# Projection products of 512 columns, issued as two matmuls of 256

## The chip, the cores and the metric

The kernel runs on one core of one Trainium2 chip. The metric is the device time of one execution in microseconds (us), and less is better. Timed runs of the kernel before gave 1808.48, 1810.51 and 1814.37 us; the median is 1810.51.

## What is computed

The program is a small encoder trunk of two layers over two requests of 512 tokens each, with 1024 features in float32. Layer 0 is differential attention, layer 1 is retention in both directions. Each layer normalizes its input, multiplies it by one wide matrix (the input projection), mixes over the tokens head by head, weighs the result with a gate and multiplies it by an output matrix. The change concerns the input projections alone:

```python
def diff_attention(h, w_in, lq1, lk1, lq2, lk2, subln_g, w_out, lambda_init):
    B, S, _ = h.shape
    proj = h @ w_in                      # 1024 x 8192
    q, k, v, gate = jnp.split(proj, [DA_QK_WIDTH, 2 * DA_QK_WIDTH, 2 * DA_QK_WIDTH + D_INNER], axis=-1)
    ...
def bidir_retention(h, w_in, decay_fwd, decay_bwd, subln_g, w_out):
    B, S, _ = h.shape
    proj = h @ w_in                      # 1024 x 6144
    q, k, v, gate = jnp.split(proj, [RET_QK_WIDTH, 2 * RET_QK_WIDTH, 2 * RET_QK_WIDTH + D_INNER], axis=-1)
    ...
```

## The kernel before

**Precision.** Matmuls run in a shortened float32 format (`float32r`). To keep the accuracy, each operand is split into a high and a low part, and each product is made of three passes, high by high, high by low and low by high: `PASSES = ((0, 0), (0, 1), (1, 0))`, where the first number picks the part of the projection weight and the second the part of the activations.

**Seven products instead of eight.** A projection is done in units, each over a block of columns of the weight and both requests. A unit multiplies blocks of two by two with seven products (`P1` to `P7`, in the order of `SEQ`) in place of eight. The activation side of them, sums and differences of the normalized inputs, is made once for a layer by `make_b` and stays in 28 slots (`Bop`): most lie in one large tile named `arena`, some in tiles of their own, which the profile shows as `b`. The weight side is made for each unit and product by `prep`: ScalarE casts the high part (line 400), VectorE subtracts for the low part (line 403), both into a `ws` tile.

**Two kinds of units.** In a *wide* unit (the value projections) the activations are the stationary operand and the weight moves past them: 128x256 matmuls in the function `wide` (line 609 of the kernel before). In a *pair* unit (queries, keys and gates) the weight is stationary, 128x128, and the activations move: one matmul of 512 columns fills a whole PSUM bank. One product of a pair unit is 4 blocks of the contraction times 3 passes, 12 matmuls of 512 columns in the function `pair` (line 599). There are 24 pair units in layer 0 and 16 in layer 1, so 40 x 7 = 280 such products. The banks they fill carry the names `pj`, `sc` and `o`. Each matmul instruction comes with its own load of the stationary operand, which the profile shows on a row of its own, PEld.

**Stages.** First comes layer 0's projection (to about 640 us), then the attention heads with layer 0's output projection (to about 1020 us), then layer 1's projection (to about 1500 us), then retention with the output projection. In the attention and retention stages other functions issue matmuls: scores (line 1116, 512 columns), attention weights times values (line 1181, 256 columns), the retention products (lines 1315, 1339, 1359, 1367, 256 columns) and the output projection (line 891, 512 columns). Lines 1028, 1040 and 1161 are transposes.

**Order.** Nothing is issued when it is written down. Every step is recorded with an engine, a cost and what it reads and writes (`plan.op`); `Plan.arrange` then simulates the engines by these costs and writes out the order on each of them. A pair product is one step of TensorE with a cost of 2.79:

```python
                    pe(2.79, lambda: pair(ps), reads, [ps])
```

In the first two units the product `P1` is issued as four steps of one contraction block each, at a cost of 0.7. A semaphore then ties a product to what it reads and to those who read its bank.

Of the kernel before, what the change touches and what calls it, by code (L numbers as in the profile page):

```python
# [253 lines left out]
def trunk_kernel(  # L254
# [7 lines left out]
    nc = tc.nc  # L262
# [90 lines left out]
    def bank(tag, name=None):  # L353
        return Buf(plan, tag, BUFS[tag], lambda i: view(pj if tag == "pj" else sc, tag, i, S, [P, S]))
# [35 lines left out]
    def pe(cost, fn, r, w, wait=0.0):  # L390
        plan.op("PE", cost, fn, r, w, wait=wait)
# [126 lines left out]
    class Unit:  # L518
# [67 lines left out]
        def product(self, op):  # L586
            which = BANK_OF[op]
            n_banks = 2 if self.wide else 1
            opens = op in OPENS
            if opens:  # L590
                self.banks[which] = [bank(self.tags[which], which) for _ in range(n_banks)]
            a, b = self.ops.pop(op), B_OF[op]
            bt = [Bop[b, k] for k in range(4)]
            reads = [q[1] for q in a] + bt

            def pair(ps, ks=range(4)):
                for k in ks:
                    for i, (u, v) in enumerate(PASSES):
                        nc.tensor.matmul(  # L599
                            ps.t, a[u][0]()[:, k, :], bt[k][:, v, :], start=(opens and k == 0 and i == 0),  # L600
                            stop=(k == 3 and i == 2), skip_group_check=True)

            def wide(ps, t):
                if self.led and op == "P1" and t == 0:
                    for j in range(NT):
                        nc.tensor.transpose(ps[:, j * P:(j + 1) * P], ident.t, ident.t)
                for k in range(4):
                    for i, (u, v) in enumerate(PASSES):
                        nc.tensor.matmul(  # L609
                            ps[:, (t % 2) * 256:(t % 2) * 256 + 256], bt[k][:, v, t * P:(t + 1) * P],  # L610
                            a[u][0]()[:, k, :], start=(opens and t % 2 == 0 and k == 0 and i == 0),
                            stop=(k == 3 and i == 2), skip_group_check=True)

            if not self.wide:
                ps = self.banks[which][0]
                if op == "P1" and self in first_units[:2]:
                    for k in range(4):
                        pe(0.7, lambda k=k: pair(ps, (k,)), reads[:2] + [bt[k]], [(ps, k)])
                else:
                    pe(2.79, lambda: pair(ps), reads, [ps])  # L620
                return
            for t in range(NT):
                ps = self.banks[which][t // 2]
                led = self.led and op == "P1" and t == 0
                pe(1.87 if led else 1.43, lambda ps=ps, t=t: wide(ps, t), reads + [ident] * led, [ps])
# [827 lines left out]
    for i in range(N2 + 1):  # L1453
        if i < N2:
            b, c = chunks[i]
# [78 lines left out]
```

## The time and the profile before

| | |
|---|---|
| timed runs, median (lowest, highest) | 1810.51 us (1808.48, 1814.37) |
| span of the profiled execution, first to last instruction | 1807.0 us |
| TensorE matmuls | 10299, busy 1794.9 us (99%) |
| weight loads | 10299, busy 1558.1 us (86%) |
| VectorE | busy 1477.1 us (82%) |
| ScalarE | busy 895.1 us (50%) |
| GpSimd | busy 169.5 us (9%) |
| DMA | 328.81 MB, mean 182 GB/s |

The profiled execution has no other time than its span; the timed runs are separate executions. Matmuls are pipelined: one starts before the one before it has ended, so the mean duration in a row (392 ns for 512 columns) is longer than the distance from start to start. A row of the timeline gives the start of a group, the time that it covers, and the count; the distance from start to start is taken from the start of one row to the start of the next.

### The profile page before, as it was taken

How to read it: one execution, taken by the hardware profiler on the slowest of the kernel's cores; microseconds unless marked ns; L12 is line 12 of the kernel's file. 1: busy time of each engine (PE TensorE's matmuls, PEld its weight loads, DVE VectorE, ACT ScalarE, POOL GpSimd, SP SyncE). 2: the span in 40 equal slices, each digit the busy share in tenths (PEclk: the TensorE clock that was granted, in tenths of full speed). 3: DMA queues.
4: the chain of work that ended last, by engine and by line, in shares of the span. 5: the costliest groups of instructions: out<-in, count | busy, mean ns of one | idle time of the engine just before them, and what ended most of it. 6: DMA issues, size and time to landing. Idle time of an engine off the chain costs nothing.

```text
span 1807.0 us, 27780 instructions
## 1 busy us (share of the span) xinstructions
PE 1794.9 (99%) x10299; PEld 1558.1 (86%) x10299; DVE 1477.1 (82%) x2319; ACT 895.1 (50%) x1856; POOL 169.5 (9%) x323
## 2 busy tenths in 40 slices
PE   9999999999999999999999999999999999999998
PEld 6789889898988888888888888898989898888887
DVE  7958787778699888888888897787887967888887
ACT  7753444433434565554555866444434355444346
POOL 1000000000000022222322300000000000111113
PEclk9999999999999999999999999999999999999999
DMA  6444455555545685444554524464657559765662
GB/s 217 134 126 137 161 140 178 184 168 155 174 126 175 201 334 198 178 156 159 190 204 140 190 73 146 140 210 146 205 156 228 151 170 396 272 238 182 225 218 94
DMA packets 162767, 328.81 MB, mean 182 GB/s; under 512 B 12724, under 2 KB 76872, under 8 KB 162632
## 3 DMA queue, kind: packets, MB, share of 16 engines
q1 hardware_dynamic: 162304, 326.71, 54.1%
q8 instruction: 81, 1.33, 0.3%
q14 instruction: 54, 0.44, 0.1%
q10 hardware_dynamic: 328, 0.34, 0.1%
HBM read 209.55 MB, written 117.44 MB: 181 GB/s over the span
## 4 chain that ended last, share of the span: by engine, by line
PE 93%; DVE 2%; DMA 2%; ACT 2%; issue 1%; POOL 0%; SPq 0%; POOLq 0%; DVEq 0%; ACTq 0%
PE pj L599 20%; PE pj L891 19%; PE sc L599 10%; PE pj L609 10%; PE o L599 8%; PE o L1181 5%; PE sc L1116 5%; PE sc L609 5%; PE o L609 2%; PE o L1359 2%; PE tp L1161 2%; PE sc L1315 1%; PE o L1367 1%; PE tp L1339 1%; DMA raw<-in_ret_w_out_dram 1%
## 5 line engine op out<-in xcount | busy, mean ns | idle before, releaser
L891 PE MATMUL pj<-ws,arena 128*128 128x512 f32 x1542 | 391.2, 397 | 0.0
L891 PEld LDWEIGHTS pj<-ws,arena 128*128 128x128 f32 x1542 | 277.7, 188 | 52.7
L599 PE MATMUL pj<-b,ws 128*128 128x512 f32 x1080 | 265.0, 392 | 0.0
L599 PEld LDWEIGHTS pj<-b,ws 128*128 128x128 f32 x1080 | 201.4, 188 | 43.0
L403 DVE TENSOR_TENSOR ws<-st,ws 128x512 fp32r<-128x512 f32 (+1 forms) x192 | 147.9, 774 | 74.8 <-ACT ws L400 56.7
L896 DVE SCALAR_TENSOR_TENSOR b<-pj,crr,b 128x512 f32<-128x512 f32 (+1 forms) x257 | 189.9, 744 | 21.4 <-PE pj L891 21.0
L403 DVE TENSOR_TENSOR ws<-raw,ws 128x512 fp32r<-128x512 f32 (+1 forms) x164 | 141.5, 868 | 71.3 <-ACT ws L400 61.0
L400 ACT CAST ws<-st 128x512 fp32r<-128x512 f32 (+1 forms) x192 | 132.4, 693 | 121.4 <-PE pj L599 36.4
L599 PE MATMUL sc<-arena,ws 128*128 128x512 f32 x768 | 186.8, 392 | 0.0
L599 PE MATMUL o<-arena,ws 128*128 128x512 f32 x744 | 180.0, 393 | 1.1 <-ACT m L385 0.6
L599 PEld LDWEIGHTS sc<-arena,ws 128*128 128x128 f32 x768 | 144.0, 188 | 31.3
L400 ACT CAST ws<-raw 128x512 fp32r<-128x512 f32 (+1 forms) x164 | 125.7, 772 | 87.0 <-PE o L599 45.0
L599 PEld LDWEIGHTS o<-arena,ws 128*128 128x128 f32 x744 | 138.4, 188 | 31.7 <-DVE arena L463 1.4
L599 PE MATMUL pj<-arena,ws 128*128 128x512 f32 x648 | 160.3, 392 | 0.4 <-DVE arena L463 0.4
L599 PEld LDWEIGHTS pj<-arena,ws 128*128 128x128 f32 x648 | 120.8, 188 | 26.7 <-DVE arena L463 0.7
L1134 ACT ACTIVATE b<-sc,nm 128x512 f32<-128x512 f32 x128 | 88.0, 689 | 66.9 <-DVE nm L1124 66.5
L636 ACT COPY c<-pj 128x512 f32<-128x512 f32 x104 | 60.9, 586 | 119.7 <-PE pj L599 66.4
L609 PE MATMUL pj<-ws,b 128*128 128x256 f32 x960 | 116.8, 276 | 0.0
L609 PEld LDWEIGHTS pj<-ws,b 128*128 128x128 f32 x960 | 113.2, 188 | 0.7
L1116 PE MATMUL sc<-arena 128*128 128x512 f32 x384 | 101.2, 395 | 0.3 <-ACT b L1134 0.3
L1181 PEld LDWEIGHTS o<-arena 128*128 128x128 f32 x768 | 93.1, 188 | 2.7
L1181 PE MATMUL o<-arena 128*128 128x256 f32 x768 | 93.7, 278 | 0.0
(207 smaller groups left out, 2855.9 us busy)
## 6 DMA issues: line engine op xcount, KB each, us to landing
qk<-os SPq DMA_DIRECT2D x192, 256.0 KB, 3.6
arena<-qk SPq DMA_DIRECT2D x96, 512.0 KB, 5.8
raw<-in_da_w_in_dram SPq DMA_DIRECT2D x64, 512.0 KB, 5.1
v<-os SPq DMA_DIRECT2D x64, 512.0 KB, 4.3
arena<-v SPq DMA_DIRECT2D x64, 512.0 KB, 4.1
raw<-in_ret_w_in_dram SPq DMA_DIRECT2D x48, 512.0 KB, 4.8
os<-g SPq DMA_DIRECT2D x32, 512.0 KB, 7.4
g<-e SPq DMA_DIRECT2D x48, 256.0 KB, 4.6
```

Of the source, the lines that this page charges most:

```text
L400: act(n, lambda: nc.scalar.copy(dst(), src()), r, w)
L403: dve(n, lambda: nc.vector.tensor_tensor(dst(), src(), hi().bitcast(F32), op=ALU.subtract), r, w)
L599: nc.tensor.matmul(ps.t, a[u][0]()[:, k, :], bt[k][:, v, :], start=(opens and k == 0 and i == 0), stop=(k == 3 and i == 2), skip_group_che ...
L609: nc.tensor.matmul(ps[:, (t % 2) * 256:(t % 2) * 256 + 256], bt[k][:, v, t * P:(t + 1) * P], a[u][0]()[:, k, :], start=(opens and t % 2 == ...
L636: act(S, lambda c=c, ps=ps: nc.scalar.copy(c.t, ps.t), [ps], [c])
L891: nc.tensor.matmul(ps[:, here], o[a][:, e, t * P:(t + 1) * P], u[b][:, e, here], start=(m == 0), stop=(m == 5))
L896: axpy(n, lambda half=half, here=here, ps=ps: nc.vector.scalar_tensor_tensor(half, ps[:, here], rr[:, t % 2:t % 2 + 1], half, op0=ALU.mult ...
L1116: nc.tensor.matmul(s.t, q[:, a, t * P:(t + 1) * P], k[:, b, :], start=(n == 0), stop=(n == 2))
L1134: act(840, lambda j=j, s=s, m=m: nc.scalar.activation(p[:, j, :], s.t, AF.Exp, bias=m.t, accum_out=sm[:, 2 * j + n:2 * j + n + 1]), [s, m] ...
L1161: nc.tensor.transpose(tp[:, j * P:(j + 1) * P], p[:, 0, j * P:(j + 1) * P], ident.t)
L1181: nc.tensor.matmul(o[:, e * 256:(e + 1) * 256], v[b][:, j, e * P:(e + 1) * P], aT[a][:, j, :], start=(n == 0), stop=(n % 12 == 11), skip_g ...
L1359: nc.tensor.matmul(o[:, e * 256:(e + 1) * 256], v_[v][:, 2 * c + j, e * P:(e + 1) * P], a_[:, u, j * 256:(j + 1) * 256], start=(e == 0 and ...
```

## The change

Each matmul of 512 columns of a pair product is issued as two of 256 columns, the left half of the bank and the right half behind each other, both with the same stationary weight. Only the very first of them clears the bank. The recorded cost of the step and all else stays as it was. The lines behind the edit have numbers higher by three in the changed kernel, and the matmul itself stands in line 601 there.

```diff
             def pair(ps, ks=range(4)):
                 for k in ks:
                     for i, (u, v) in enumerate(PASSES):
-                        nc.tensor.matmul(
-                            ps.t, a[u][0]()[:, k, :], bt[k][:, v, :], start=(opens and k == 0 and i == 0),
-                            stop=(k == 3 and i == 2), skip_group_check=True)
+                        for c in range(2):
+                            here = slice(c * 256, (c + 1) * 256)
+                            nc.tensor.matmul(
+                                ps[:, here], a[u][0]()[:, k, :], bt[k][:, v, here],
+                                start=(opens and k == 0 and i == 0 and c == 0),
+                                stop=(k == 3 and i == 2), skip_group_check=True)
```

## The prediction

> **What bounds the kernel now.** I read the busy times first, then the chain that ended last, then the waits of TensorE, then the timeline of single stretches.
>
> ```profile
> span 1807.0 us, 27780 instructions
> PE 1794.9 (99%) x10299; PEld 1558.1 (86%) x10299; DVE 1477.1 (82%) x2319; ACT 895.1 (50%) x1856; POOL 169.5 (9%) x323
> PEclk9999999999999999999999999999999999999999
> ...
> PE 93%; DVE 2%; DMA 2%; ACT 2%; issue 1%; POOL 0%; SPq 0%; POOLq 0%; DVEq 0%; ACTq 0%
> ```
>
> TensorE is busy for 99% of the span, and 93% of the chain that ended last is TensorE. Its granted clock is full in every slice. There are as many weight loads (PEld) as matmuls, 10299 of each. The waits of TensorE on others, longest first in total, are no more than 1.4 us in any row:
>
> ```profile
> PE sc L1010 <- DVE minus L411: 1.4, 1, 1.4
> PE tp L1028 <- DVE arena L463: 1.0, 2, 0.7
> ```
>
> So what counts is the pitch of the matmuls, from start to start; the mean duration of one overlaps with the next and can't be added up. In the groups by line with shapes kept apart, the matmuls that the change touches are all of line 599:
>
> ```profile
> L599 PE MATMUL pj<-b,ws 128*128 128x512 f32 x1080 | 265.0, 392 | 0.0
> L599 PE MATMUL sc<-arena,ws 128*128 128x512 f32 x768 | 186.8, 392 | 0.0
> L599 PE MATMUL o<-arena,ws 128*128 128x512 f32 x744 | 180.0, 393 | 1.1 <-ACT m L385 0.6 <-DVE arena L463 0.3
> L599 PE MATMUL pj<-arena,ws 128*128 128x512 f32 x648 | 160.3, 392 | 0.4 <-DVE arena L463 0.4
> L599 PE MATMUL sc<-b,ws 128*128 128x512 f32 x120 | 29.1, 391 | 0.0
> ```
>
> That is 1080 + 768 + 744 + 648 + 120 = 3360 matmuls of 512 columns, 280 products of 12. Their pitch is read from a stretch of the timeline that holds nothing else. Between these rows lie 16 further products of 12 (two of them shown as 6 + 6):
>
> ```profile
> 207.10 2.91 PE L599 MATMUL sc<-arena,ws 128*128 128x512 f32 x12
> ...
> 253.79 2.91 PE L599 MATMUL pj<-b,ws 128*128 128x512 f32 x12
> 256.54 2.91 PE L599 MATMUL o<-arena,ws 128*128 128x512 f32 x12
> ```
>
> From 207.10 to 256.54 are 18 products, 216 matmuls in 49.44 us: **228.9 ns each**. That holds while VectorE is at 94% (below), so it is TensorE's own pace.
>
> **The change, part by part.** Each of the 3360 matmuls becomes two of 256 columns, with the same stationary tile `ws`, the two halves of the moving tile, and the two halves of the bank. It adds 3360 matmuls and 3360 weight loads (13659 of each after it). Whether the loads of equal weights are merged can be read off what is there: the first two passes of a product already use the same high part of the weight, and the page still counts a load for each matmul. So I take it that each half loads.
>
> The order of the other instructions is the same on every engine in the changed program, since the planner's cost of a product, 2.79, is left as it was. Nothing is moved past a queue and no wait is added; only the time of the 280 products can change.
>
> The trace shows the new shape already. The wide units (line 609) issue 128x256 matmuls with a new weight for each, in the same stages and at the same background of the other engines:
>
> ```profile
> 303.18 5.60 PE L609 MATMUL sc<-ws,arena 128*128 128x256 f32 x48
> 308.62 0.84 PE L609 MATMUL pj<-ws,b 128*128 128x256 f32 x6
> ...
> 314.06 5.60 PE L609 MATMUL sc<-ws,arena 128*128 128x256 f32 x48
> 319.50 5.60 PE L609 MATMUL pj<-ws,b 128*128 128x256 f32 x48
> ```
>
> From 303.18 to 308.62 are 48 of them in 5.44 us, and from 314.06 to 319.50 again 48 in 5.44 us: **113.3 ns each**, so 226.7 for two halves against 228.9 for the whole. But there is a second pitch for this shape. The products of attention weights with values (line 1181) run at one of two paces, with the same shape and the same two tiles:
>
> ```profile
> 707.12 2.99 PE L1181 MATMUL o<-arena 128*128 128x256 f32 x24
> 709.95 1.56 PE L1116 MATMUL sc<-arena 128*128 128x512 f32 x6
> ...
> 719.37 2.90 PE L1181 MATMUL o<-arena 128*128 128x256 f32 x24
> 722.10 1.08 PE L1116 MATMUL sc<-arena 128*128 128x512 f32 x4
> ```
>
> The first group takes 2.83 us for 24, **117.9 ns each**; the second 2.73 us, 113.8. And in the retention stage, two lines in which, as here, two matmuls behind each other use the same weight:
>
> ```profile
> 1594.42 0.86 PE L1339 MATMUL tp<-arena 128*128 128x256 f32 x6
> 1595.12 0.87 PE L1315 MATMUL sc<-arena 128*128 128x256 f32 x6
> 1595.82 1.54 PE L891 MATMUL pj<-ws,arena 128*128 128x512 f32 x6
> ```
>
> Both take 0.70 us for 6, 116.7 ns each, in groups too short to settle. Neither row has TensorE waiting, so the slower pace lies in how a weight load and the running matmul get on with each other. Which pace the new products keep is the whole question, and the trace of before can't show it: there the stationary tile is `ws` and the moving one is the arena or `b`, at 512 columns only.
>
> The bounds for a pair of halves are thus 226.7 and 2 x 117.9 = 235.8 ns against 228.9: a gain of 2.2 or a loss of 6.9 ns for each old matmul. Of the 3360, those of the start don't set the pace:
>
> ```profile
> core 0: us, PE busy (x) PEld busy (x), PEclk, DMA share, GB/s
> 0.00:50.00 50.00, 29.59 (x120) 21.89 (x120) 1.00 0.57 196
> ```
>
> These 120 fall in the first 50 us, where TensorE has gaps before new operands. I count the other 3240. The fast pace gives 3240 x 2.2 ns = -7.2 us, the slow one 3240 x 6.9 ns = +22.4 us. **I take the fast pace**: line 609 is the nearest row, being in the same stages, with the same two kinds of tiles in changed roles, and its pace holds: from 303.18 to 319.50 it issues 144 matmuls (eight groups of 6 lie between the rows) in 16.32 us. Only its first 48 behind a product of line 599 take 0.03 us longer, in the chain in order of time:
>
> ```profile
> 297.87 5.47 PE o L609 x48
> 303.34 5.44 PE sc L609 x48
> ```
>
> Such a crossing stays in one form or another, some 24 times: at most 0.7 us either way, which I leave at nothing.
>
> What covers the rest? The other engines first: a faster TensorE asks more of VectorE. The windows of a stretch of pair products alone and of one of mostly wide products:
>
> ```profile
> 500.00:600.00 100.00, 100.00 (x439) 82.04 (x438) 93.96 (x152) 40.12 (x71) 0.00 (x0) 1.00 0.48 143
> 299.00:327.00 28.00, 28.00 (x241) 27.63 (x239) 19.66 (x31) 12.20 (x21) 0.00 (x0) 1.00 0.57 175
> ```
>
> The columns after the length are the busy times of PE, PEld, DVE, ACT and POOL. VectorE has 6 us free in 100, and TensorE would take 1 us less for the same work, so it stays ahead; were that cover gone, no more than the 7.2 us of gain would go with it. The loader is at 82% in the first stretch and at 99% in the second: line 609 runs at 113.3 ns with the loader filled, so a filled loader is no bar by itself. Does its reading slow others? The same VectorE operation in both stretches, pair products first:
>
> ```profile
> L403 DVE TENSOR_TENSOR ws<-st,ws 128x512 fp32r<-128x512 f32 x21 | 14.4, 685 | 1.3 <-ACT ws L400 0.8
> ...
> L403 DVE TENSOR_TENSOR ws<-st,ws 128x512 fp32r<-128x512 f32 x3 | 2.0, 682 | 0.0
> ```
>
> 685 and 682 ns: no. And the fetching of 6720 more instructions:
>
> ```profile
> q8 instruction: 81, 1.33, 0.3%
> ```
>
> The columns are packets, MB, and their share of the time of 16 engines. 81 packets of 16 KB are, if they are TensorE's 10299 loads and as many matmuls, some 250 instructions each. At two instructions in 113.3 ns a packet lasts 14 us, and 0.3% of 16 engines' span is 1.1 us for each: hidden, at nothing. If it weren't, each of some 26 new packets would cost about that 1.1 us, 29 us in all; the 144 matmuls of line 609 above are more than a packet holds and pass without a gap, so I don't count it.
>
> The sum against the profiled execution: 1807.0 - 7.2 = 1799.8 us of span. The median of the runs, 1810.51, lies 3.5 us above the span, for what is around it and the spread of runs (1808.48 to 1814.37). So 1810.5 - 7.2 = **1803.3 us**.
>
> **The rivals.**
>
> *The slow pace* (slower). A load that starts just behind the start of a matmul and reads at the same time holds that matmul up by 4.6 ns, at every one of them, since each half now has a load beside its whole length, where a 512-column matmul has the second part of its length free of it. Place: every pair product in both projection stages. For it: line 1181 keeps 117.9 over a whole group of 24, and lines 1315 and 1339, which repeat a weight as the halves do, are above 113.3. Against it: line 609, with a load beside every matmul too, falls back to 113.3 each time. It decides from a mean pitch of 114.4 ns, half of 228.9. Price: +22.4 us, **1832.9 us**. I give it 0.20.
>
> *A price for each matmul in between*, by changing between both paces or by a small start-up cost of each instruction: a mean of (113.3 + 117.9) / 2 = 115.6 ns, 231.2 for two, 2.3 more than now, x 3240 = +7.5 us: **1818 us**. For it: the 116.7 ns of the two retention lines. Against it: two matmuls of line 609 cost less than one of line 599, which leaves no room for a price per instruction. I give it 0.17.
>
> The Trainium skill speaks for this one: "TensorE: Matmul & The Clock Gate", section "Back-to-back issue gap", gives a warm matmul N / 2.4 + 2.5 ns, so a fixed part that twice as many matmuls pay twice. By that rule (an estimate from its figures) the halves would cost 2.5 ns more than the whole, 3240 times, +8.1 us, 1818.6 us. The trace disagrees on both lengths: 228.9 where the rule has 215.8, and 113.3 where it has 109.2, and the difference that it makes has the other sign.
>
> *No change*: the second half goes without its load, or the pitch is per column after all. Two matmuls at half of 228.9 each: 1810.5 us. For it: 226.7 and 228.9 are within 1%. Against it: loads of equal weights are not merged now. 0.05.
>
> **How the numbers follow.** The fast pace keeps 0.58. About 0.3%, 5.4 us, is what a measurement of this kernel can tell from no change. The gain of 7.2 us is only 1.8 us beyond that, less than the spread of the runs, so I put one in six of the fast case within it: faster 0.48; within 0.3% 0.10 + 0.05 = 0.15; slower 0.20 + 0.17 = 0.37. The fast case alone would be 1800 to 1806. The range has to reach to the others, until little is left out: from 1800 to the slow pace and a little spread above, 1834.
>
> **What would show it right or wrong.** Right: 13659 matmuls and loads; a product of 24 halves in 2.72 us from start to start in the middle of a stretch, where it was 2.75; the loader near 100% in 500 to 600 us; no new waits of TensorE; the lines of the attention and retention stages as before. Slow pace: 2.83 us a product in long stretches. In between: some stretches at 2.72 and others at 2.83. Wrong in another way: new idle time before the loads (instructions or operands late), or a longer mean of the VectorE operations beside the filled loader.

## The result, and the profile after

The changed kernel takes 1825.70 us (median of 5, 1825.36 to 1827.21), the kernel before in the same comparison 1808.48 us (median of 5, 1808.26 to 1814.37). The ratio is 1.0093, with a 95% interval of 1.0081 to 1.0104: slower by 17 us, where 7 us faster was forecast. The profiled execution has a span of 1823.4 us, 16.4 more than before; the granted clock is 0.999 in both.

From the page of the changed kernel, the span, the busy times, the queue that brings the instructions, and the chain by engine:

```profile
span 1823.4 us, 34495 instructions
...
PE 1812.6 (99%) x13659; PEld 1716.5 (94%) x13659; DVE 1478.1 (81%) x2319; ACT 895.6 (49%) x1856; POOL 170.0 (9%) x323
...
q8 instruction: 107, 1.75, 0.4%
...
PE 93%; DVE 2%; DMA 2%; ACT 1%; issue 0%; POOL 0%; SPq 0%; POOLq 0%; DVEq 0%; ACTq 0%
```

TensorE is still what counts, with the 13659 matmuls and loads that were foreseen. Its longest wait is the one of before, and VectorE's operation beside the pair products takes what it took; a row of the waits, and one of the groups from 500 to 600 us:

```profile
PE sc L1013 <- DVE minus L411: 1.4, 1, 1.4
```

```profile
L403 DVE TENSOR_TENSOR ws<-st,ws 128x512 fp32r<-128x512 f32 x21 | 14.4, 685 | 3.9 <-ACT ws L400 3.7
```

So the time went into the pitch, the distance from one matmul's start to the next one's. Two pieces of the timeline of the changed kernel, both with nothing but pair products (columns: start, time covered, engine, line, operation, count):

```profile
213.60 2.99 PE L601 MATMUL pj<-b,ws 128*128 128x256 f32 x24
216.42 2.99 PE L601 MATMUL pj<-arena,ws 128*128 128x256 f32 x24
219.25 2.99 PE L601 MATMUL pj<-b,ws 128*128 128x256 f32 x24
...
506.54 2.88 PE L601 MATMUL pj<-b,ws 128*128 128x256 f32 x24
509.26 2.88 PE L601 MATMUL pj<-arena,ws 128*128 128x256 f32 x24
511.98 2.88 PE L601 MATMUL pj<-b,ws 128*128 128x256 f32 x24
```

From 213.60 to 219.25 are 48 halves in 5.65 us, 117.7 ns each (117.8 over longer pieces); from 506.54 to 511.98 are 48 in 5.44 us, 113.3 ns each. Same line, tiles of the same names, VectorE busy for 85% beside both pieces: **two paces, each held for a long stretch**. Going through all starts of the trace, 4944 of the 6720 halves belong to stretches at 117.8 ns and 1776 to stretches at 113.3. Where a stretch changes its pace stands in the chain in order of time (start, length, engine, bank, line, count; L612 are the wide products):

```profile
158.37 5.66 PE pj L612 x48
164.03 2.83 PE pj L601 x24
166.86 5.45 PE o L612 x48
...
188.63 5.44 PE pj L612 x48
196.79 5.66 PE pj L612 x48
202.45 2.83 PE o L601 x24
```

The wide product at 158.37 is slow (5.66 for 48) and so is the pair product behind it (2.83 for 24). The next wide product, at 166.86, is fast (5.45) and stays so. Between the end of the row at 188.63 (194.07) and 196.79 lies a pair product of 2.72, fast as well; and the wide one behind that, at 196.79, is slow again, as is the pair product at 202.45. So, in this trace, **the pace goes over unchanged from wide to pair, and turns into the other one from pair to wide**. In the whole of it 24 of 24 entries into pair products keep the pace, and 20 of 23 entries into wide ones turn it (the three others lead to 12 wide matmuls ahead of a transpose). Five wide stretches come directly behind transposes; all five are slow here. The stretch that a turn begins can be long: 792 halves from 202.45 on, 1224 up to 634 us.

By the sum of all distances from start to start, the pair line went from 774.3 to 787.0 us (+12.7) and the wide line, which the change doesn't touch, from 305.7 to 309.9 (+4.1 before rounding). Together 16.8, against 16.4 of span. The rest of the program moved by less than half a microsecond.

### The profile page after: what moved, and what is told of

The parts are those of the page before. It is cut to its first block, busy times and chain, and to the rows that moved or that the text cites. A ratio compares the mean times of both kernels' runs of the same rounds, so it can differ in the third digit from the quotient of the medians.

```text
span 1823.4 us, 34495 instructions
## 1 busy us (share of the span) xinstructions
PE 1812.6 (99%) x13659; PEld 1716.5 (94%) x13659; DVE 1478.1 (81%) x2319; ACT 895.6 (49%) x1856; POOL 170.0 (9%) x323
## 4 chain that ended last, share of the span: by engine, by line
PE 93%; DVE 2%; ACT 2%; DMA 1%; issue 0%; POOL 0%; SPq 0%; POOLq 0%; DVEq 0%; ACTq 0%
PE pj L601 21%; PE pj L894 18%; PE sc L601 11%; PE pj L612 10%; PE o L601 8%; PE o L1184 5%; PE sc L612 5%; PE sc L1119 5%; PE o L612 2%; PE o L1362 2%; PE tp L1164 2%; PE sc L1318 1%; PE o L1370 1%; PE tp L1342 1%; DMA raw<-in_ret_w_out_dram 1%; DVE ws L403 1%
## 5 line engine op out<-in xcount | busy, mean ns | idle before, releaser
L601 PE MATMUL pj<-b,ws 128*128 128x256 f32 x2160 | 269.3, 279 | 0.0
L601 PEld LDWEIGHTS pj<-b,ws 128*128 128x128 f32 x2160 | 259.4, 188 | 0.3
L601 PE MATMUL sc<-arena,ws 128*128 128x256 f32 x1536 | 189.8, 279 | 0.0
L601 PE MATMUL o<-arena,ws 128*128 128x256 f32 x1488 | 183.6, 279 | 1.0 <-ACT m L385 0.6
L601 PEld LDWEIGHTS sc<-arena,ws 128*128 128x128 f32 x1536 | 183.6, 188 | 0.0
L601 PEld LDWEIGHTS o<-arena,ws 128*128 128x128 f32 x1488 | 178.0, 188 | 2.0 <-DVE arena L463 1.1
L601 PE MATMUL pj<-arena,ws 128*128 128x256 f32 x1296 | 162.5, 278 | 0.4 <-DVE arena L463 0.4
L601 PEld LDWEIGHTS pj<-arena,ws 128*128 128x128 f32 x1296 | 155.7, 188 | 0.9 <-DVE arena L463 0.6
L612 PE MATMUL pj<-ws,b 128*128 128x256 f32 x960 | 118.6, 278 | 0.0
L612 PEld LDWEIGHTS pj<-ws,b 128*128 128x128 f32 x960 | 114.3, 188 | 0.0
```

The costliest lines, as they stand in the source:

```text
L601: nc.tensor.matmul(ps[:, here], a[u][0]()[:, k, :], bt[k][:, v, here], start=(opens and k == 0 and i == 0 and c == 0), stop=(k == 3 and i ...
L612: nc.tensor.matmul(ps[:, (t % 2) * 256:(t % 2) * 256 + 256], bt[k][:, v, t * P:(t + 1) * P], a[u][0]()[:, k, :], start=(opens and t % 2 == ...
```

## The experiments

The questions were: what makes the two paces, what changes between them, and whether the loss belongs to the change as such. The expectations quoted here number the theories as they came up and say in themselves what each means. The kernel before took 1808.6 to 1809.3 us (medians) beside them. Where an interval is given, a kernel ran 4 to 11 times; e1, e2, e5 to e7, e10, e11 and e13 to e16 are one execution each.

**e1: is it the repeated weight?** The halves no longer stand behind each other: 12 left ones, then 12 right ones, so that a weight comes back only 12 matmuls later.

```diff
-                for k in ks:
-                    for i, (u, v) in enumerate(PASSES):
-                        for c in range(2):
+                for c in range(2):
+                    for k in ks:
+                        for i, (u, v) in enumerate(PASSES):
```

> The two halves of a bank are no longer behind each other: a product issues its 12 matmuls for the left half, then its 12 for the right half, so the weight repeats only where the passes repeat it anyway (4 of 12 steps, as in the kernel before) and not 8 of 12. Theory 1 (a stretch of 256-column matmuls holds one of two paces, 113.3 or 117.8 ns, whatever the weights; which one is set by how the stretch was entered and flips where a wide product follows a pair product): both paces again in long stretches, time between 1803 and 1833 us, near the changed kernel's 1825. Theory 2 (a load of the weight that is loaded already, directly behind its first load, costs 4.5 ns): the pair products keep 113.3 to 115 ns throughout, time 1803 to 1812 us.

Measured: 1822.83 us. From the chain in order of time, a piece of the first long stretch and one of the last of layer 0:

```profile
131.88 8.16 PE pj L601 x72
...
499.34 8.48 PE pj L601 x72
```

8.16 / 72 = 113.3 ns and 8.48 / 72 = 117.8: both paces, in long stretches, exchanged against those of the changed kernel. Again 20 of 23 entries from pair to wide turn the pace and none from wide to pair does. 4356 halves are at the slow pace, 588 fewer than in the changed kernel; 588 x 4.5 ns = 2.6 us, and the time is 2.9 below its median. A repeated weight is not the cause: the wide products, whose stationary part is another one at every matmul, run at 117.8 ns too. And the paces account for the time.

**e2, e5, e6: what turns the pace?** In 38 of the 40 pair units, extra matmuls into the bank that the product clears anyway: in e2 six with the roles exchanged (activations stationary, weight moving), in e5 six with the roles of the pair products, in e6 a single exchanged one.

```diff
             def pair(ps, ks=range(4)):
+                if opens and op == "P1" and 0 in ks and len(ks) == 4:
+                    for j in range(6):
+                        nc.tensor.matmul(
+                            ps[:, 0:256], bt[j % 4][:, 0, 0:P], a[0][0]()[:, 0:2, :],
+                            start=True, stop=True, skip_group_check=True)
```

> Ahead of the product P1 of 38 of the 40 pair units stand six added 256-column matmuls with the roles exchanged (activations stationary, weight moving), whose result the opening matmul of the product clears. They cost 38 x 6 x about 115 ns = 26 us by themselves. Theory 1 (the pace is a held state that flips at a crossing from pair to exchanged roles): the pace of the pair products changes between 113.3 and 117.8 ns at these places, stretches of about one unit in length, near half of the pair products at each; 1826 + 26 - 8 = about 1844 us. Theory 2 (repeated weights): the pair products keep their pace across the added ones, 1826 + 26 = 1852 us.

> Control to the kernel with added matmuls of exchanged roles: at the same 38 places six added 256-column matmuls, but with the roles of the pair products (weight stationary, activations moving); the opening matmul clears their result. If the exchange of roles is what flips the pace, the pair products keep their pace across these places, and the pace changes only at wide products and behind transposes; 1826 + 26 = 1852 us give or take what the entries make of it (1835 to 1860). If any break in the sequence of a product flips it, the pace changes at the added matmuls.

> At the same 38 places one added 256-column matmul with exchanged roles instead of six. If the flip is made at the crossing itself, one is enough and the pace changes at each place as with six; 38 x 0.115 = 4 us of added work, 1825 + 4 - 8 = about 1822 us. If the new pace has to be found over several matmuls of the exchanged kind, one does not flip it and the pair products keep their pace, about 1830 us.

Measured: 1849.13, 1851.27 and 1842.17 us. The timeline of e2 (added matmuls L599, pair products L606), then that of e5 in the same place:

```profile
115.83 2.99 PE L606 MATMUL sc<-b,ws 128*128 128x256 f32 x24
118.66 0.86 PE L599 MATMUL pj<-ws,arena 128*128 128x256 f32 x6
119.35 2.88 PE L606 MATMUL pj<-arena,ws 128*128 128x256 f32 x24
122.07 2.88 PE L606 MATMUL sc<-b,ws 128*128 128x256 f32 x24
...
138.39 0.87 PE L599 MATMUL pj<-ws,arena 128*128 128x256 f32 x6
139.10 2.99 PE L606 MATMUL pj<-arena,ws 128*128 128x256 f32 x24
141.93 2.99 PE L606 MATMUL pj<-b,ws 128*128 128x256 f32 x24
```

```profile
115.43 2.99 PE L606 MATMUL sc<-b,ws 128*128 128x256 f32 x24
118.26 0.87 PE L599 MATMUL pj<-arena,ws 128*128 128x256 f32 x6
118.97 2.99 PE L606 MATMUL pj<-arena,ws 128*128 128x256 f32 x24
121.79 2.99 PE L606 MATMUL sc<-b,ws 128*128 128x256 f32 x24
```

Before the six exchanged matmuls of e2 the pair products are slow (2.83 from 115.83 to 118.66), behind them fast (2.72 from 119.35 to 122.07), behind the next six slow again (2.83 from 139.10 to 141.93). Of its 25 insertions into a run of pair products all 25 turn the pace; of the 25 of e5 none does. So it is the exchange of roles that turns it, and not the six added matmuls as such. The pace turns as theory 1 has it, but the time of e2 is nearer to the 1852 us of theory 2 than to the 1844 of theory 1, because the shares of both paces differ from those assumed: against the changed kernel it has about 1190 slow halves fewer, 620 slow wide matmuls more and 228 added ones of some 0.12 us, about 1850 us by these prices.

One exchanged matmul isn't enough to reach the fast pace: in e6 all 24 insertions into slow products leave them slow, the one into fast products makes them slow, and 6492 of the 6720 halves end up at 117.8. Neither of its two expected times came. The run also limits the rule read from the changed kernel's trace: of its 23 entries from pair to wide only 14 turn the pace, and nine, all from slow groups of 24 halves, stay slow. One of the nine, in the chain in order of time of e6 (between the two wide products lies a pair product of 2.81, from 163.79 to 166.60):

```profile
158.13 5.66 PE pj L616 x48
166.60 5.65 PE o L616 x48
```

So the pace alone doesn't fix what the next exchange does; what else does isn't known. The added time of e6 follows from the paces: against the changed kernel 1548 slow halves and 1308 slow wide products more at 4.5 ns, and 38 matmuls of some 0.12 us, 17.4 us in all, to 1843; measured 1842.17.

**e7: is it the length of the load?** The right half loads 64 columns of the weight only, so this kernel leaves out half of the output rows of the right halves.

```diff
+                            m = 64 if c == 1 and not (opens and k == 0 and i == 0) else P
                             nc.tensor.matmul(
-                                ps[:, here], a[u][0]()[:, k, :], bt[k][:, v, here],
+                                ps[0:m, here], a[u][0]()[:, k, 0:m], bt[k][:, v, here],
```

> The right half of each bank is computed for 64 of the 128 output rows only (its stationary tile has 64 columns; the first matmul that opens a bank keeps 128), so every second load is half as long; the other 64 rows of the right halves are left out. If the slow pace is the load's reading beside the running matmul, the left halves, beside which the short load runs, come down from 117.8 to 113 to 116 ns in slow stretches, and the right halves stay. If the length of the load does not count, both stay at 117.8 in slow stretches and at 113.3 in fast ones.

Measured: 1826.49 us. Groups of the loader from 500 to 600 us, then the timeline of the same stretch:

```profile
L602 PEld LDWEIGHTS pj<-b,ws 128*128 128x128 f32 x150 | 28.1, 187 | 0.0
...
L602 PEld LDWEIGHTS pj<-b,ws 128*64 128x64 f32 x150 | 20.1, 134 | 0.0
```

```profile
500.44 2.99 PE L602 MATMUL sc<-arena,ws 128*128 128x256 f32 x24
503.27 2.98 PE L602 MATMUL pj<-b,ws 128*128 128x256 f32 x24
506.09 2.98 PE L602 MATMUL pj<-arena,ws 128*128 128x256 f32 x24
```

The short load takes 134 ns in place of 187, and the slow pace stays: 48 halves from 500.44 to 506.09 in 5.65 us, 117.7 ns in the mean. By the single starts the two halves are no longer alike in such a stretch: 116.6 ns from a left half, beside which the short load runs, to the right one, and 118.9 from there to the next left half, 235.5 for both, where it was 235.6; in a fast stretch both take 113.3. So the length of the load moves time from one half to the other, but a load shortened beside every second matmul doesn't end the slow pace. Short loads throughout were not tried.

**e3, e4: is it the alignment of the tiles?** A constant of one column is put into another tile, so that all TensorE operands lie 32 bytes lower, at multiples of 64; e3 is the changed kernel, e4 the one before.

```diff
-    minus1 = const([P, 1], "minus1")
+    minus1 = Buf(plan, "minus1", 1, lambda i: gcol[:, 24:25])
```

> The changed kernel with one small constant column moved into another tile, so that every tile that TensorE reads starts 32 bytes lower in its partition, on a multiple of 64 bytes instead of 32 beside it; nothing else changes. Theory 3 (the two paces come from how the load's and the matmul's reads fall into 64-byte lines; 256 columns from 32 beside a line touch 17 lines, and 113.3 ns is 17 times 6.67 ns): 256 columns touch 16 lines, the pace falls to 107 to 112 ns for all 256-column matmuls, and the kernel to 1720 to 1800 us. Theory 1 with paces that hang on the relative places of the two tiles alone, which stay: the same two paces, 1826 us within what the entries make of it (1803 to 1833).

> The kernel before with the same shift by 32 bytes. Theory 3: the 512-column matmuls fall from 228.9 to 214 to 224 ns and the kernel to 1700 to 1785 us. Theory 1: 228.9 ns as before, 1810 us within 0.3%.

Measured: 1824.42 us (1821.45 to 1827.34), ratio 1.0093 (1.0076 to 1.0109); and 1809.63 us (1807.80 to 1814.52), ratio 1.0005 (0.9996 to 1.0014). Both paces are there as before, and whole matmuls stay at 229 ns. Moving both operands together by 32 bytes changes neither, which speaks against theory 3.

**e8, e9, e12: can the fast pace be kept?** In the kernel before, wide products come behind whole matmuls of 512 columns and run at 113.3 ns. So e8 takes whole matmuls for the product just ahead of a wide one and for the first one behind anything that isn't pair or wide, halves for all others (600 whole, 5520 halves). e9 takes halves only where the stretch was entered from a wide product (3432 halves); e12 is e9 once more.

```diff
+                ahead, then = plan.around
+                parts = 1 if then == "wide" or not plan.settled else 2
+                n = S // parts
                 for k in ks:
                     for i, (u, v) in enumerate(PASSES):
-                        for c in range(2):
-                            here = slice(c * 256, (c + 1) * 256)
+                        for c in range(parts):
+                            here = slice(c * n, (c + 1) * n)
```

(`plan.around` holds the kinds of the steps before and behind on TensorE, `plan.settled` whether a wide product came first in the stretch; in e8 the condition is `then == "wide" or ahead == "other"`.)

> Halves only where the fast pace should hold: a pair product is issued as 12 whole matmuls of 512 columns where the next step of TensorE is a wide product or the last one was neither pair nor wide, and in halves otherwise (230 of 280 products). In the kernel before, all 22 entries from 512 columns into wide products ended at 113.3 ns after five matmuls. Theory 1 (the state is set by the entry; from 512 columns it is the fast one, and from wide to pair it is kept): nearly all halves at 113.3 ns, 5520 of them, so -(2760 x 2.2) = -6.1 us, some 20 entries at 0.03 us more: 1803 to 1806 us. Rival (an entry from 512 columns leads pair halves into the slow pace, since load and moving tile have exchanged places): stretches behind transposes and the rest at 117.8, 1815 to 1829 us.

> Halves only in stretches that are entered from a wide product: a pair product is whole (512 columns) until a wide product has run since the last step that is neither pair nor wide, and whole again where the next step is wide; 3432 halves stand for 1716 whole matmuls. Theory 1 (the wide products, entered from 512 columns, are fast, and the pace is kept from wide to pair): all 3432 halves at 113.3 ns, wide products as in the kernel before, -(1716 x 2.2) = -3.8 us: 0.998 of the kernel before, about 1805 us, with fewer differences from run to run than the hybrid before. Rival (what the halves gain at 113.3 ns is lost at entries and elsewhere, as the hybrid's ratio of 1.0003 could be read): 1.000.

> The same kernel as e9_behind_wide, once more, for an interval: whole 512-column products in every stretch that is entered from a start, a transpose or another kind of product, 256-column halves only in the stretches of pair units that are entered from a wide product. Theory (the place of the two operands admits both paces, and entry from a wide product that runs at the fast one leaves the halves at 113.3 ns): 3432 halves, 1716 pairs, times 228.9 minus 226.7 ns is 3.8 us less than the kernel before, so a ratio of 0.998 with an interval wholly below 1. Rival (the entry does not decide, the stretches of e9 were at the fast pace by chance): some stretches come at 117.8 ns in other executions, each about 100 us long costing 100/117.8 x 4.5 ns = 3.8 us, so times from 1805 up to 1812 and a ratio whose interval holds 1.

Measured: e8 1809.12 us (1807.38 to 1812.28), ratio 1.0003 (0.9994 to 1.0012); e9 1805.23 us, ratio 0.9989 (0.9969 to 1.0009); e12 1805.59 us, ratio 0.9988 (0.9968 to 1.0008). A piece of the first long stretch of e8, entered from a transpose; then e9, behind wide products:

```profile
61.19 5.81 PE L609 MATMUL o<-arena,ws 128*128 128x256 f32 x48
66.85 5.34 PE L609 MATMUL pj<-b,ws 128*128 128x256 f32 x44
```

```profile
504.14 2.88 PE L612 MATMUL o<-arena,ws 128*128 128x256 f32 x24
506.86 2.88 PE L612 MATMUL sc<-arena,ws 128*128 128x256 f32 x24
```

In e8 the first long stretch is slow (5.66 us for 48), and so are short ones behind transposes, which takes back most of the gain of the rest in the profiled execution (1807.38 us); in e9 all halves run at 113.3 ns (2.72 for 24), in the profiled executions of e9 and of e12. The medians are 3.5 and 3.6 us below the kernel before, where 3.8 were worked out. But of the 21 timed executions two took 1823.95 and 1822.40 us, the others 1804.53 to 1806.32, and the intervals hold 1: lower in 19 of 21, not shown to be lower on the mean. No trace covers one of the two long ones; if all its halves went at the slow pace, that would be 3432 x 4.5 ns = 15 us of the 17 to 19.

**e10, e11: is it where the operands lie to each other?** In the program as built, each weight tile `ws` begins 192 bytes behind the activation tiles, counted modulo 512 bytes within a partition: the slots begin 32 elements into the `arena` tile, which is 80 elements longer than its 18 slots, and the working tiles follow it, so 48 elements of four bytes remain; the tiles `b` have the same remainder as the slots. The slots in the arena (not those named `b`) are put 64 bytes lower in e10 (distance 256) and 128 lower in e11 (distance 320).

```diff
-        lo = 32 + at * 1024 + shift
+        lo = 16 + at * 1024 + shift
```

(That is e10; in e11 the 16 is left out as well.)

> The changed kernel with the slots of the large arena tile 64 bytes lower, while the weight tiles and the activations in tiles of their own stay: the distance between the two operands of a pair product changes by 64 bytes for most products and not for those that read b. Theory 1 with paces that belong to TensorE's own beat: the same two paces, flips at the crossings as before, 1820 to 1833 us. Theory 4 (the slow pace is a collision of the two reads in the same part of the memory, given by their distance): products that read the arena change their pace, to 113.3 or to above 117.8 ns, and those that read b do not.

> As the run with 64 bytes, with the slots 128 bytes lower. Theory 1: the same two paces, 1820 to 1833 us. Theory 4: the pace of products that read the arena differs from that of products that read b.

Measured: 1858.45 and 1826.86 us. The timelines, e10 and then e11:

```profile
517.21 2.99 PE L601 MATMUL pj<-b,ws 128*128 128x256 f32 x24
520.04 3.05 PE L601 MATMUL pj<-arena,ws 128*128 128x256 f32 x24
522.93 2.99 PE L601 MATMUL pj<-b,ws 128*128 128x256 f32 x24
```

```profile
505.66 2.89 PE L601 MATMUL pj<-arena,ws 128*128 128x256 f32 x24
508.39 2.99 PE L601 MATMUL pj<-b,ws 128*128 128x256 f32 x24
511.21 2.89 PE L601 MATMUL o<-arena,ws 128*128 128x256 f32 x24
513.94 2.88 PE L601 MATMUL sc<-arena,ws 128*128 128x256 f32 x24
```

In e10 the product that reads the arena takes 2.89 us from 520.04 to 522.93, 120 ns a matmul, the one that reads `b` before it 2.83, 117.9. In e11 it is the other way round: 2.73 with the arena, twice (113.8 ns), 2.82 with `b` (117.5), side by side in the same stretch. The same instruction on data of the same size, and only the place of one operand differs. In the long stretches of e11 all but the first products that read the arena take 113.3 to 114.4 ns a matmul; in short stretches, behind transposes and between wide products some still take 117.5 or more.

**e13 to e18: and is it the change, or the place?** e13 and e14 try other distances (128 for both kinds; 64 for `b` with 128 for the arena). e15 and e16 are the kernel before at the places of e11 and e13; e17 and e18 repeat e11 and e15 with an interval. The edit of e13 is shown; in e14 the tile has 48 in place of 80, with the slots of e10.

```diff
-    arena = ar.tile([P, 18 * 1024 + 80], F32R, tag="arena", name="arena")
+    arena = ar.tile([P, 18 * 1024 + 64], F32R, tag="arena", name="arena")
```

> The changed kernel with the arena tile 64 bytes shorter, so that all working tiles behind it, the weight tiles ws among them, lie 64 bytes lower: the distance from a moving activation tile to its weight tile, modulo 512 bytes, becomes 128 for every pair product (192 before), and 384 the other way round for the wide ones (320 before). Theory 4 (the distance alone decides which paces there are): a pitch of the pair products that is one of the three seen or a new one, the same for those that read the arena and those that read b; if the two-pace place is a single distance, a single pace in all stretches, at 113.3 ns 1801 us, at 120.0 ns 1853 us for the pair lines alone. Rival (64 bytes change nothing unless they bring the distance to 256): both paces in long stretches as now, 1825 us.

> The changed kernel with the working tiles 128 bytes lower and the arena's slots 64 bytes lower: distance 64 for the pair products that read b, 128 for those that read the arena (192 for both before). Theory 4: the products that read the arena go as in e13, and those that read b have a pace of their own, visible side by side in each stretch. Rival: no difference between the two kinds in one stretch, both paces in long stretches as in the changed kernel, 1825 us.

> The kernel before (512 columns) with the arena's slots 128 bytes lower, as in e11, whose difference to it is then the change alone at that place. If the place only matters for matmuls of 256 columns, the pair products stay at 228.9 ns, the wide products and the output projection lose what they lost in e11 (wide products that read the arena up to 2 ns each x 1728 = 3 us, output projection 2.2 ns x 1530 = 3.4 us): 1815 us, and e11 is 12 us above it, because its products that read b (2400 of the 6720) run at 117.8 ns in part. If the place matters for 512 columns as well, the pair products show another pitch than 228.9, up to 2 x 120.0 ns, and the time is 1820 to 1845 us.

> The kernel before with the working tiles 64 bytes lower, as in e13, whose difference to it is then the change alone at that place. If the place leaves 512 columns alone: 228.9 ns, 1809 us. If the wide products have another pace at 384 than at 320: up to 2688 x 4.5 ns = 12 us more.

> The kernel of e11 (the changed kernel, arena's slots 128 bytes lower) once more, beside e18. Theory 4: at this place the change costs nothing, since the products that read the arena keep 113.3 ns and 226.7 of two halves stands against 233 of the whole matmul: 1826 to 1828 us, a ratio to e18's within 0.3% of 1. Rival (e11 and e15 were near each other by chance, the change costs about 15 us everywhere): 15 us above e18.

> The kernel of e15 (512 columns, arena's slots 128 bytes lower) once more, beside e17. Theory 4: 1826 to 1828 us. Rival: 1812 us.

Measured: e13 1852.63, e14 1843.44, e15 1827.24, e16 1837.64 us. The timelines, e15 (whole matmuls at distance 320 and 192), e13 and e16 (distance 128, halves and whole), e14 (64 with `b`):

```profile
503.14 2.91 PE L599 MATMUL pj<-b,ws 128*128 128x512 f32 x12
505.89 2.95 PE L599 MATMUL pj<-arena,ws 128*128 128x512 f32 x12
508.68 2.91 PE L599 MATMUL pj<-b,ws 128*128 128x512 f32 x12
```

```profile
512.67 3.01 PE L601 MATMUL sc<-arena,ws 128*128 128x256 f32 x24
515.52 3.01 PE L601 MATMUL pj<-b,ws 128*128 128x256 f32 x24
```

```profile
508.93 2.96 PE L599 MATMUL pj<-b,ws 128*128 128x512 f32 x12
511.72 2.95 PE L599 MATMUL pj<-arena,ws 128*128 128x512 f32 x12
```

```profile
511.86 2.89 PE L601 MATMUL pj<-b,ws 128*128 128x256 f32 x24
514.60 3.01 PE L601 MATMUL pj<-arena,ws 128*128 128x256 f32 x24
517.45 2.99 PE L601 MATMUL pj<-b,ws 128*128 128x256 f32 x24
520.27 3.01 PE L601 MATMUL o<-arena,ws 128*128 128x256 f32 x24
```

e15: 2.75 us with `b`, 229 ns a matmul, and 2.79 with the arena, 232.5. e13: 2.85 for 24, 118.8 ns. e16: 2.79 for 12, 232.5 ns. e14: with `b` 2.74 and 2.82 (114.2 and 117.5 ns), with the arena 2.85 in between. The arena products of e14 and those of e13 lie at addresses 64 bytes apart with the same distance, 128, and take the same 2.85 us: with e3 and e4 that speaks for the distance and against the address of one operand alone. The means over all starts of the pair line, without the distances of 300 ns and more, in which it waits or other work lies:

| distance of weight to activations | two halves | whole | change gives |
|---|---|---|---|
| 192, as built | 226.7 or 235.6, held (mean 234) | 229.1 | 17 us slower |
| 320 (e17, e18, arena) | 228 to 230 | 232 to 233 | 0.9 us slower, see below |
| 128 (e13, e16) | 238 | 232.4 | 15.0 us slower |
| 256 (e10, arena) | 240 to 241 | not run | not run |
| 64 (e14, `b`) | 231 in the mean, of both paces | not run | not run |

e17 took 1827.66 us (1826.61 to 1829.24) and e18 1826.74 us (1826.33 to 1826.91): ratios to the kernel before of 1.0105 (1.0088 to 1.0121) and 1.0096 (1.0081 to 1.0111). They are 0.9 us apart (0.05%), and the intervals overlap. **So the same change costs 17 us at one place of the operands and nothing that can be told apart at another**, where the products that read the arena, 4320 of the 6720 halves, have the new distance. By the sums from start to start, the products that read the arena take 9.6 us less in e17 than in e18, those that read `b`, still at distance 192, 7.3 more, and the wide ones 2.3 more. Both kernels are slower than the kernel before as built, since whole matmuls are dearer at 320, and so are the wide products and the output projection (362.1 us by its starts as built, 365.6 in both).

## Why the prediction was wrong, by its steps

**What held.** The count of matmuls and loads and that equal weights are loaded twice; no new wait; VectorE beside a filled loader (685 ns before and after); the instruction fetch: 107 packets, 26 more as worked out, and no time for them. Both prices of a half held to 0.1 ns: 113.3 and 117.8, where 113.3 and 117.9 were read off lines 609 and 1181. Of the signs named beforehand, the one in between is what came: "some stretches at 2.72 and others at 2.83".

**The step that failed** is "I take the fast pace: line 609 is the nearest row ... and its pace holds". The reading was right and the reason for it was missing. In the kernel before, 23 of the 28 stretches of line 609 are entered from 512-column matmuls and five from transposes, and all 28 settle at 113.3 ns. Behind 256-column halves it mostly takes the other pace from theirs, and holds that one just as well: the same line is at 117.8 ns in 1044 of its 2688 matmuls after the change. The five stretches behind transposes are fast before and slow after the change, with the same transposes directly ahead, so what decides can lie further back than the neighbour; how isn't shown. A pace that holds in all examples may be a state that all examples enter in the same way; the two paces of line 1181, in the very rows quoted, said that there are two.

**The crossing** was priced at 0.7 us at most and left at nothing. By itself it does cost next to nothing. But it decides the pace of the next stretch, up to 1224 halves at 4.5 ns, 5.5 us each. It had been read as a price where it is a switch.

**The lines that the change leaves alone** were taken as unchanged. The wide line lost 4.1 us of the 16.8, because its pace now depends on that of the pair products ahead of it; "only the time of the 280 products can change" was wrong by that.

**The sum.** In place of 3240 x -2.2 ns = -7.2 us there are, with the two prices and the counts of the trace, 4944 x 117.8 + 1776 x 113.3 - 3360 x 229.1 ns = +13.9 us for the pair line (+12.7 measured, since the gaps beside the paces, mainly at the start and behind transposes, fell from 4.5 to 3.4 us), and 4.1 for the wide one. The measured 1825.70 us lies in the range that was given only because the range was drawn out to the rivals.

**The rivals.** *The slow pace* had the right size for each matmul, and it was right in 74% of the halves; its mechanism, the load that holds the running matmul up over its length, doesn't fit e7, where a load shorter by 53 ns beside every second matmul leaves the time of the two halves together as it was, and its condition, a mean pitch over 114.4 ns, came true for the mean (117) and not for every stretch. *In between* had the right form, changing between both paces, with half the halves at each; the true share was 74%, and it missed the wide line. That its rule from the Trainium skill ("TensorE: Matmul & The Clock Gate", section "Back-to-back issue gap") gives 2.5 ns more for two halves than for the whole isn't borne out: the trace has 2.4 less in one stretch and 6.5 more in another. That section of the Trainium skill gives the rule for a matmul that stands alone and says that in a stream of loads and matmuls both set the spacing, which the prediction left out. *No change* did not come for the reason given there: both halves load, and the pitch is not per column.

## What to carry to other kernels

When a row shows the pace of an instruction, look for what precedes it in every example: a pace that was only seen in one sequence is evidence for that sequence, not for the instruction alone. Before an edit that changes the length of matmuls, look for two paces of one shape anywhere in the trace, and count as touched all lines that border on the changed ones. And where a change of matmul shape comes out wrong, it can be worth trying at another place of the operands: a verdict of 17 us can be one on the addresses. No place tried here made the changed kernel faster than the kernel before as built.

## What the runs showed of the hardware

In the kernel as built, matmuls of 256 columns with a load each run, without any wait, at one of two paces, 113.3 or 117.8 ns, and keep it for up to 1224 matmuls. An exchange of the roles of both tiles for six matmuls turns one into the other (25 of 25 insertions in e2), six matmuls without exchange don't (0 of 25 in e5), and a single exchanged one doesn't lead from slow to fast (0 of 24 in e6).

Which paces there are depends on where both operands lie to each other within the partition: 64 bytes take the halves from 113.3 or 117.8 to 120 ns (e10), 128 bytes to 113.3 to 114.4 in the long stretches (e11), at distances of 256 and 320 modulo 512. Whole matmuls change too, 229.1 to 233 (e15). The Trainium skill, "TensorE: Matmul & The Clock Gate", section "Step-by-step: what each phase is for", says that the weight load and the moving operand have read ports of their own, so that loading the next weights takes no read bandwidth from the running matmul. What this case shows is that the place of the two operands to each other changes the time, 113.3 against 120 ns for the same matmul; whether that is their reading getting in each other's way isn't shown.

Open are: what in the chip makes two paces at a distance of 192; why a stretch behind a transpose mostly, and not always, begins at the slow one (slow in the first long stretch of the changed kernel, fast in that of e1 and e3); why nine entries of e6 don't turn the pace; what distances the runs leave out would give; and the two long executions of e9 and e12, of which there is no trace.
